# Way out of the first two FFN chunks as seven half products, placed among the way in of the next chunk

## The chip, the cores and the metric

The kernel runs on one core of one Trainium2 chip. The metric is the device time of one execution in microseconds (us); the time quoted for a kernel is the median of its timed runs. Five engines work side by side: TensorE (PE, matmuls; PEld is its loading of weights), VectorE (DVE), ScalarE (ACT), GpSimd (POOL) and SyncE (SP). DMA transfers are issued here by SP (plain loads) and by POOL (among them all that add what they bring onto what lies in SBUF). Each engine executes its own queue in order and waits on semaphores.

## The reference, cut to what matters

```python
D_MODEL, SEQ, DEPTH, D_FF = 1024, 512, 2, 2816

def swiglu(h, w_in, w_out):
    gate, up = jnp.split(h @ w_in, 2, axis=-1)
    return (jax.nn.silu(gate) * up) @ w_out

def reference(...):
    for l in range(DEPTH):
        x = x + 0.5 * swiglu(rms_norm(x, ffn1_norm[l]), ffn1_w_in[l], ffn1_w_out[l])
        h = rms_norm(x, mix_norm[l]) @ w_mix_in[l]
        ...
        x = x + y @ w_mix_out[l]
        x = x + 0.5 * swiglu(rms_norm(x, ffn2_norm[l]), ffn2_w_in[l], ffn2_w_out[l])
    return x
```

There are four FFNs in all. Everything is float32. Only the FFNs are touched by the change; the three mixers between them are not.

## The kernel before

x is held transposed in SBUF as `xT`: 8 tiles of 128 features by 512 tokens. An FFN has 2816 inner features, 22 blocks of 128, in three chunks of 8, 8 and 6 blocks (`CHUNKS`). "Way in" is the product with w_in (1024 rows; gate and up columns), "way out" the product with w_out.

**Precision.** Every float32 operand is split into a high part (an ACT cast to fp32r, line 196) and a low part (a DVE subtract, line 197), and each product is three matmuls, high by high, high by low, low by high (`mm3`, lines 208, 212, 213). `parted` splits a piece of 128x1024 weights into one of three `hl` buffers.

**Way in.** The first blocks of an FFN (`covered`: 6, in the first FFN of layer 1 4) are computed plainly in `cover`, while the normalisation is worked out. All others are done in `halved`, two blocks at a time (a *unit*), by Strassen's scheme in Winograd's form: with two columns of blocks (gate, up) by two halves of the 1024 rows by two halves of the tokens, seven half products P1 to P7 take the place of eight. Their factors are sums: of the normalised x, made once per FFN (`halves_of_x`, 14 tiles `xh*`, `xl*`), and of quarters of w_in, made per unit. A unit loads four quarters of 512 KB (line 529, SP, tiles `x0` to `x7`, two units' worth). Its sums are made by two accumulating transfers from DRAM (lines 532 and 541, POOL), one DVE add into a tile `S` (line 537), and one accumulating transfer from `S` in SBUF (line 545). A half product is 24 matmuls over 256 columns, 8 per group of three, into one PSUM bank; the weights of a half product are split two half products ahead (`LEAD`). After it comes one step of putting together on ACT or DVE (lines 597 to 619): copies out of PSUM, adds, SiLU, the products gate by up (`y`), which are split at once into `hh` and `hl`.

**Way out.** After each chunk's way in, `ffn` computes the way out of the chunk plainly: two halves of the output features, four banks each, over the chunk's inner blocks; w_out is staged by SP in pieces `st` of 512 KB (line 177), split, and multiplied in matmuls over 512 columns. After each half four DVE operations (line 370) add half of the banks to `xT`. In the last chunk the normalisation of the next stage, or the transposition of the output, hangs on this.

**Order.** The order of the instructions on each engine follows the order of the program text closely, with a scheduler's shifts at compile time. PSUM has 8 banks: `mm` 3, `sc` 2, `pt` 2, `po` 1; consecutive units and output halves take the one four and the other in turn.

Of the kernel before, what the change touches and what calls it, by code (L numbers as in the profile page):

```python
# [8 lines left out]
F32 = mybir.dt.float32  # L9
# [14 lines left out]
P = 128  # L24
T = 512
# [6 lines left out]
CHUNKS = ((0, 8), (8, 8), (16, 6))  # L32

# [11 lines left out]
class Trunk:  # L45
# [32 lines left out]
    def build_consts(self, scratch):  # L78
# [3 lines left out]
        self.ones_r = c.tile([1, P], F32, tag="ones_r", name="ones_r")  # L82
# [231 lines left out]
    def ffn(self, w_in, w_out, next_gain, covered, begin=None, out=None):  # L314

        nc = self.nc
        tc = self.tc
        with tc.tile_pool(name=self.n("ffn"), bufs=1) as fp:  # L320
            self.tt, self.tb = "g2", 2
            if begin is not None:
                x, gain, logits = begin
            for f0, nf in CHUNKS:
                self.hh = [
                    fp.tile([P, 2, T], F32R, tag=f"hh{q}", name=self.n("hh")) for q in range(nf // 2)
                ]
                self.hl = [
                    fp.tile([P, 2, T], F32R, tag=f"hl{q}", name=self.n("hl")) for q in range(nf // 2)
                ]  # L330
                halved = self.halved(fp, w_in, f0 + (covered if f0 == 0 else 0), f0 + nf, f0)
                finish = self.cover(fp, w_in, covered, begin, halved) if f0 == 0 else None
                for n, _ in enumerate(halved):

                    if f0 == 0 and n == 0:
                        finish()
                final = f0 + nf == NFF
                if final and next_gain is not None:
                    self.begin_norm(next_gain)
                last = final and out is not None  # L340
                if last:
                    xs = self.turn_x()
                for dg in range(2):
                    banks = self.next4()

                    def parts(k, kk, dg=dg):
                        r = slice((f0 + k) * P, (f0 + k + kk) * P)
                        return [w_out[r, dg * 512 : (dg + 1) * 512]]

                    spans = [slice(c, c + P) for c in (0, 128, 256, 384)]  # L350
                    self.stream(
                        [
                            (bk, slice(0, T), c) if last else (bk, c, None)
                            for bk, c in zip(banks, spans)
                        ],
                        parts, lambda k: (self.hh[k // 2][:, k % 2, :], self.hl[k // 2][:, k % 2, :]), nf,
                    )
                    if last:
                        for i in range(4):
                            o = self.xo[dg * 4 + i]  # L360
                            nc.vector.scalar_tensor_tensor(
                                out=o, in0=banks[i], scalar=0.5, in1=xs[dg * 4 + i],
                                op0=ALU.mult, op1=ALU.add,
                            )
                            nc.sync.dma_start(out[0, spans[i], dg * T : (dg + 1) * T], o)
                        continue
                    for i in range(4):
                        j = dg * 4 + i
                        xj = self.xT[:, j, :]
                        nc.vector.scalar_tensor_tensor(  # L370
                            out=xj, in0=banks[i], scalar=0.5, in1=xj,
                            op0=ALU.mult, op1=ALU.add,
                        )
                        if final and next_gain is not None:
                            self.norm_part(j, fp)

    def cover(self, fp, w_in, covered, begin, then):
# [7 lines left out]
        for f in range(0, covered, 2):  # L385
# [22 lines left out]
            if opening and begin is not None:  # L408
                nt = iter(["xh4", "xl4", "xh5", "xl5", "xh6", "xl6", "hh2", "hl2", "hh3", "hl3"])
                self.build_consts(lambda dt: fp.tile([P, T], dt, tag=next(nt), name=self.n("c")))  # L410
                self.lower_bounds(logits)
                norm()
# [16 lines left out]
    def finish(self, fp, f, i, pg, pu):  # L429
# [7 lines left out]
        nc.vector.tensor_mul(ui, gi, ui)  # L437
        hh, hl = self.hh[f // 2][:, i, :], self.hl[f // 2][:, i, :]
        nc.scalar.copy(hh, ui)
        nc.vector.tensor_sub(hl, ui, hh)  # L440

    def halves_of_x(self, fp):
# [7 lines left out]
        for q in range(4):  # L450
            xq = fp.tile([P, 2, T], F32, tag=("hh2", "hl2", "hh3", "hl3")[q], name=self.n("xn"))
# [41 lines left out]
        t1 = both(fp.tile([P, 4, H], F32, tag="S", name=self.n("T"), bufs=3))  # L493
# [9 lines left out]
    def halved(self, fp, w_in, fa, fb, f0):  # L503
# [10 lines left out]
        ORDER = ("P1", "P2", "P6", "P5", "P7", "P3", "P4")  # L514
        steps = [(f, p) for f in range(fa, fb, 2) for p in ORDER]
        raw, sums, parts = {}, {}, {}

        def quarter(f, q):
            c = (q // 2) * FF + f * P
            return w_in[(q % 2) * 512 : (q % 2) * 512 + 512, c : c + 2 * P].rearrange(  # L520
                "(k p) c -> p k c", p=P
            )

        def load(f):
            for q in (2, 3, 0, 1):
                t = self.res.tile(
                    [P, 4, 2 * P], F32, tag=f"x{4 * ((f - fa) // 2 % 2) + q}", name=self.n("w")
                )
                nc.sync.dma_start(t, quarter(f, q))
                raw[f, q] = t  # L530

            nc.gpsimd.dma_start(raw[f, 2], quarter(f, 3), accum_op=ALU.add)

        def second(f):

            t = sums[f] = fp.tile([P, 4, 2 * P], F32, tag="S", name=self.n("S"), bufs=3)
            nc.vector.tensor_add(t, raw[f, 2], raw[f, 0])

        def third(f):

            nc.gpsimd.dma_start(raw[f, 0], quarter(f, 2), accum_op=ALU.add)

        def fourth(f):

            nc.gpsimd.dma_start(raw[f, 1], sums[f], accum_op=ALU.add)

        def prepare(f, p):
            src = {
                "P1": raw[f, 0], "P2": raw[f, 1], "P6": sums.get(f), "P5": raw[f, 2],
                "P7": raw[f, 0], "P3": raw[f, 1], "P4": raw[f, 3],  # L550
            }[p]
            hi, lo = self.parted(src.rearrange("p k c -> p (k c)"), skew=SKEW_HELD)
            parts[f, p] = [a.rearrange("p (k c) -> p k c", k=4) for a in (hi, lo)]

        def product(f, p, bank, first, last, parted):
            hi, lo = parts.pop((f, p))
            xh, xl = self.xc[p]
            for i in range(2):
                acc, c = bank[:, i * H : (i + 1) * H], slice(i * P, (i + 1) * P)
                for k in range(4):  # L560
                    self.mm3(
                        acc, hi[:, k, c], lo[:, k, c], xh[:, k, :], xl[:, k, :],
                        first and i == 0 and k == 0, last and i == 1 and k == 3,
# [4 lines left out]
        LEAD = 2  # L568
        load(fa)
        for f, p in steps[:LEAD]:  # L570
            prepare(f, p)
        yield
        for n, (f, p) in enumerate(steps):
            if p == "P1" and f == fa:
                second(f)
            if p == "P1":
                third(f)
                fourth(f)
            if n + LEAD < len(steps):
                prepare(*steps[n + LEAD])  # L580
            if f + 2 < fb:
                if p == "P1":
                    load(f + 2)
                elif p == "P7":
                    second(f + 2)
            if p == "P1":
                self.ntog += 1
                a, b, c = (
                    self.bank(t) for t in (("mm", "mm", "mm"), ("sc", "sc", "pt"))[self.ntog % 2]
                )  # L590
            product(
                f, p, {"P2": c, "P5": b, "P3": b}.get(p, a), p in ("P1", "P2", "P5"),
                p in ("P2", "P3", "P4"), n == 0,
            )
            if p == "P1":
                g1 = tmp("g1")
                nc.scalar.activation(g1, a, AF.Copy, scale=-1.0)
            elif p == "P2":
                nc.vector.tensor_add(g1, g1, c)
                self.act(g1, g1, AF.Silu)  # L600
            elif p == "P6":
                g2 = tmp("g2")
                nc.scalar.activation(g2, a, AF.Copy, scale=-1.0)  # L603
            elif p == "P5":
                u2 = tmp("u2")
                nc.scalar.activation(u2, b, AF.Copy, scale=-1.0)
            elif p == "P7":
                nc.vector.tensor_add(u2, u2, a)
            elif p == "P3":
                nc.vector.tensor_add(g2, g2, b)  # L610
                self.act(g2, g2, AF.Silu)
            else:
                q = (f - f0) // 2
                pair = lambda t: t.rearrange("p (i t) -> p i t", i=2)
                y = fp.tile([P, 2, T], F32, tag="S", name=self.n("y"), bufs=3)
                nc.vector.tensor_mul(y[:, :, H:], pair(g2), pair(u2))
                nc.vector.tensor_mul(y[:, :, :H], pair(g1), pair(a))
# [725 lines left out]
```

## Time and profile before

| | us |
|---|---|
| median of 3 runs | 1919.83 (1919.29 to 1922.33) |
| the profiled execution | 1915.45 |
| its span, first to last instruction | 1913.7 |
| mean granted TensorE clock | 0.997 |

| stretch of the first FFN | us |
|---|---|
| first chunk: covered blocks and one halved unit | 0 to 108.9 |
| its way out | 108.9 to 152.3 |
| second chunk: four units of the way in | 152.3 to 228.8 |
| its way out | 228.8 to 272.3 |
| third chunk: three units | 272.3 to 329.4 |
| its way out | 329.4 to 362.1 |

The other FFNs have the same stretches (the first of layer 1 has one unit more in its first chunk). A page of the profile has the busy time of each engine, 40 slices of the span, the DMA queues, the chain of work that ended last, and the costliest groups of instructions. Durations of matmuls overlap, since matmuls are pipelined: what counts for TensorE is the distance from start to start. In the DMA figures a share of 1 means that the packets' times add up to the time of all 16 DMA engines.

### The profile page before, as it was taken

The page shows a single profiled execution, that of the slowest core. Times are in us where ns is not written, and L with a number is a line of the kernel's source. Part 1 is how long each engine was busy: PE and PEld are TensorE (multiplying, and loading weights), DVE is VectorE, ACT ScalarE, POOL GpSimd, SP SyncE. Part 2 cuts the span into 40 slices and gives each one's busy share as a digit, 9 for nine tenths or more (in the row PEclk, how much of TensorE's full clock was granted, in tenths as well). Part 3 has the DMA queues.
Part 4 walks back from the last instruction along what each step waited for, and adds up shares of the span by engine and source line. Part 5 has one row for each costly group of instructions (what it writes and reads, how often), then busy time and mean ns, then how long its engine had stood idle before and what let it go on. Part 6 is the DMA issues. An engine that isn't in the chain of part 4 may idle for free.

```text
span 1913.7 us, 30445 instructions
## 1 busy us (share of the span) xinstructions
PE 1879.9 (98%) x12240; PEld 1683.8 (88%) x12240; DVE 1280.2 (67%) x1905; ACT 928.9 (49%) x1422; POOL 142.3 (7%) x155
## 2 busy tenths in 40 slices
PE   8999999999999999999999999999999999999999
PEld 6889989899877788989989899998998787899897
DVE  7856646578787864755687466566868878656463
ACT  4434535464666542534555254355646664335252
POOL 0101100100000010201001010101000000111010
PEclk9999999999999999999999999999999999999999
DMA  5747734232323384855349376523323234858442
GB/s 143 189 142 158 193 101 99 72 94 70 78 75 93 101 229 110 195 148 111 89 146 211 105 184 170 121 72 78 89 67 84 78 101 132 207 123 202 116 100 89
DMA packets 215661, 237.56 MB, mean 124 GB/s; under 512 B 19264, under 2 KB 184128, under 8 KB 215520
## 3 DMA queue, kind: packets, MB, share of 16 engines
q1 hardware_dynamic: 175408, 183.69, 31.6%
q0 software_dynamic: 40112, 51.93, 16.9%
q8 instruction: 96, 1.57, 0.3%
q14 instruction: 45, 0.37, 0.1%
HBM read 210.87 MB, written 2.10 MB: 111 GB/s over the span
## 4 chain that ended last, share of the span: by engine, by line
PE 83%; DVE 8%; DMA 4%; ACT 3%; issue 2%; SPq 0%; POOL 0%; POOLq 0%; ACTq 0%; DVEq 0%
PE mm L208 13%; PE mm L213 13%; PE mm L212 13%; PE sc L208 8%; PE sc L212 8%; PE sc L213 8%; PE pt L208 4%; PE pt L212 4%; PE pt L213 4%; DMA w<-in_ffn_w_in_dram 3%; PE po L208 2%; PE po L213 2%; PE po L212 2%; DVE hl L197 1%; DVE xc L487 1%
## 5 line engine op out<-in xcount | busy, mean ns | idle before, releaser
L196 ACT CAST hl<-st 128x512 fp32r<-128x512 f32 (+2 forms) x268 | 222.4, 832 | 375.5 <-PE pt L213 113.0
L197 DVE TENSOR_TENSOR hl<-st,hl 128x512 fp32r<-128x512 f32 (+2 forms) x268 | 254.9, 952 | 219.0 <-ACT hl L196 217.9
L197 DVE TENSOR_TENSOR hl<-w,hl 128x1024 fp32r<-128x1024 f32 x198 | 242.6, 1226 | 228.6 <-ACT hl L196 228.4
L196 ACT CAST hl<-w 128x1024 fp32r<-128x1024 f32 x198 | 207.0, 1045 | 195.1 <-PE po L213 52.7
L208 PE MATMUL mm<-xc,hl 128*128 128x256 f32 (+1 forms) x958 | 265.3, 278 | 7.0 <-ACT g L603 7.0
L213 PE MATMUL mm<-xc,hl 128*128 128x256 f32 x952 | 265.0, 278 | 5.3 <-DVE hl L197 5.3
L212 PE MATMUL mm<-xc,hl 128*128 128x256 f32 x952 | 264.8, 278 | 0.0
L208 PE MATMUL sc<-xc,hl 128*128 128x256 f32 (+1 forms) x774 | 212.4, 276 | 0.0
L212 PE MATMUL sc<-xc,hl 128*128 128x256 f32 x768 | 212.3, 276 | 0.0
L213 PE MATMUL sc<-xc,hl 128*128 128x256 f32 x768 | 212.1, 276 | 0.0
L208 PEld LDWEIGHTS mm<-xc,hl 128*128 128x128 f32 x958 | 181.5, 189 | 8.3 <-ACT g L603 7.8
L213 PEld LDWEIGHTS mm<-xc,hl 128*128 128x128 f32 x952 | 180.3, 189 | 5.8 <-DVE hl L197 5.7
L212 PEld LDWEIGHTS mm<-xc,hl 128*128 128x128 f32 x952 | 180.2, 189 | 0.0
L208 PEld LDWEIGHTS sc<-xc,hl 128*128 128x128 f32 x774 | 145.3, 188 | 0.5
L212 PEld LDWEIGHTS sc<-xc,hl 128*128 128x128 f32 x768 | 144.2, 188 | 0.0
L213 PEld LDWEIGHTS sc<-xc,hl 128*128 128x128 f32 x768 | 144.2, 188 | 0.0
L208 PE MATMUL mm<-hl,x 128*128 128x256 f32 (+1 forms) x384 | 112.6, 293 | 0.7 <-DVE ft L298 0.4
L208 PE MATMUL mm<-x,hl 128*128 128x512 f32 x272 | 109.6, 403 | 0.0
L213 PE MATMUL mm<-hl,x 128*128 128x256 f32 (+1 forms) x384 | 107.7, 280 | 0.0
L212 PE MATMUL mm<-hl,x 128*128 128x256 f32 (+1 forms) x384 | 107.4, 280 | 0.0
L213 PE MATMUL mm<-x,hl 128*128 128x512 f32 x272 | 106.4, 391 | 0.0
L212 PE MATMUL mm<-x,hl 128*128 128x512 f32 x272 | 105.9, 389 | 0.0
(411 smaller groups left out, 4502.2 us busy)
## 6 DMA issues: line engine op xcount, KB each, us to landing
w<-in_ffn_w_in_dram SPq DMA_DIRECT2D x132, 512.0 KB, 5.1
st<-in_ffn_w_out_dram SPq DMA_DIRECT2D x88, 512.0 KB, 3.3
w<-in_ffn_w_in_dram POOLq DMA_DIRECT2D x66, 512.0 KB, 6.8
st<-in_ffn_w_in_dram SPq DMA_DIRECT2D x88, 256.0 KB, 3.1
st<-in_w_mix_in_dram SPq DMA_DIRECT2D x88, 256.0 KB, 2.7
w<-S POOLq DMA_DIRECT2D x33, 512.0 KB, 6.0
st<-in_w_mix_out_dram SPq DMA_DIRECT2D x24, 256.0 KB, 2.6
st<-in_w_mix_in_dram SPq DMA_DIRECT2D x32, 128.0 KB, 2.4
```

Of the source, the lines that this page charges most:

```text
L196: a = nc.scalar.copy(hi, src[:, c : c + w])
L197: b = nc.vector.tensor_sub(lo, src[:, c : c + w], hi)
L208: nc.tensor.matmul(acc[:, c], ah, bh[:, c], start=first and c.start == 0, stop=False, skip_group_check=True,)
L212: nc.tensor.matmul(acc, ah, bl, start=False, stop=False, skip_group_check=True)
L213: nc.tensor.matmul(acc, al, bh, start=False, stop=last, skip_group_check=True)
L487: nc.vector.tensor_sub(l, u, h)
```

## The change

The way out of chunks 0 and 1 is no longer a stage of its own. It is computed in two groups (`("O", (c, g))`, c the chunk, g the group: 256 columns of each half of w_out's 1024), each by seven half products of the same form as the way in: two halves of the chunk's 1024 inner features by two halves of the output by two halves of the tokens. `halved` now runs over the whole FFN; its list `seq` strews the 14 half products of chunk c among those of the way in of chunk c+1: 42 half products in the first mixed stretch, 35 in the second. The last chunk's way out stays as it was.

- **Inner values.** The products gate by up of chunks 0 and 1 are no longer split when made. They go into four quarters per chunk (`quarter`, 128 x 4 x 256). `moving` splits the sum that each P needs (7 per chunk, into `mh`, `ml`); the sums themselves are made by four accumulating transfers per chunk from SBUF to SBUF (`add_hidden`).
- **w_out.** Each group loads four quarters of 512 KB in turn into the tiles `x0` to `x7`, which it shares with w_in, and its sums are made by four accumulating transfers from DRAM (`add`). Its splits are those of `prepare`, seven per group.
- **xT.** After each of the 14 half products one DVE operation adds its bank to (or subtracts it from) a quarter of a group's part of `xT`. For P1, P6, P7 and P4, and for P5 and P3, the bank goes on accumulating in between.
- **Plan.** Loads and sums are issued by a table `todo`, filled ahead: at half product n the splits for n + 2, then sums on DVE, inner splits, loads, transfers that add. A load is issued 4 half products ahead of the split that needs it (`AHEAD_LOAD`), a first sum 4 ahead (`AHEAD_SUM`); later sums one half product after the split of the contents that they replace.
- **First unit of an FFN.** Its three sums that were transfers (lines 532, 541, 545) are made by DVE (`at_once`).
- `S` has two buffers and not three; `lower_bounds` works in a piece of a buffer at hand; `ones_r` is 1x1; way-in and way-out half products each take four of the PSUM banks in turn.

```diff
+ORDER_IN = ("P1", "P2", "P6", "P5", "P7", "P3", "P4")
+ORDER_OUT = ("P2", "P1", "P5", "P6", "P7", "P3", "P4")
+LEAD = 2
+AHEAD_LOAD, AHEAD_SUM = 4, 4
...
-            for f0, nf in CHUNKS:
...
-                halved = self.halved(fp, w_in, f0 + (covered if f0 == 0 else 0), f0 + nf, f0)
...
+            halved = self.halved(fp, w_in, w_out, covered)
+            finish = self.cover(fp, w_in, covered, begin, halved)
+            for n, _ in enumerate(halved):
+                if n == 0:
+                    finish()
+            f0, nf = CHUNKS[-1]
...
+        into = lambda c: [
+            ("I", f, p) for f in range(max(covered, c[0]), c[0] + c[1], 2) for p in ORDER_IN
+        ]
+        outof = lambda c: [("O", (c, g), p) for p in ORDER_OUT for g in range(2)]
+        seq = into(CHUNKS[0])
+        for c, pattern in ((0, "IIIO" + "IIO" * 12 + "IO"), (1, "IIIO" + "IOIIO" * 6 + "O")):
+            ii, oo = iter(into(CHUNKS[c + 1])), iter(outof(c))
+            seq += [next(ii if k == "I" else oo) for k in pattern]
...
+        def load(u, q, tag):
+            raw[u, q] = t = self.res.tile([P, 4, 2 * P], F32, tag=f"x{tag}", name=self.n("w"))
+            nc.sync.dma_start(t, src(u, q))
+        def add(u, q, q2):
+            nc.gpsimd.dma_start(raw[u, q], src(u, q2), accum_op=ALU.add)
+        def add_second(u):
+            nc.gpsimd.dma_start(raw[u, 1], sums[u], accum_op=ALU.add)
+        def at_once(u, name):
+            a, b, c, op = {
+                1: lambda: (raw[u, 2], raw[u, 2], raw[u, 3], ALU.add),
+                3: lambda: (raw[u, 0], sums[u], raw[u, 3], ALU.subtract),
+                4: lambda: (raw[u, 1], raw[u, 1], sums[u], ALU.add),
+            }[name]()
+            nc.vector.tensor_tensor(a, b, c, op=op)
...
+        def moving(c, p):
+            t = self.quarter(fp, c, *SUM[p])
+            hi, lo = (
+                fp.tile([P, 4, H], F32R, tag=f"m{w}", name=self.n("m"), bufs=2) for w in "hl"
+            )
+            if p in ("P1", "P7", "P4"):
+                nc.scalar.activation(hi, t, AF.Copy, scale=-1.0)
+                nc.vector.scalar_tensor_tensor(
+                    out=lo, in0=t, scalar=-1.0, in1=hi, op0=ALU.mult, op1=ALU.subtract
+                )
+            else:
+                nc.scalar.copy(hi, t)
+                nc.vector.tensor_sub(lo, t, hi)
+            mov[c, p] = hi, lo
+        def add_hidden(c, x, y):
+            x, y = (self.quarter(fp, c, *q) for q in (x, y))
+            nc.gpsimd.dma_start(x, y, accum_op=ALU.add)
...
+            split = {p: at[kind, w, p] - LEAD for p in ORDER_IN}
+            if kind == "I":
...
+                    when(m - AHEAD_SUM, 5, add, u, 2, 3)
+                    when(m, 2, second, u)
+                    when(max(m, split["P1"]), 5, add, u, 0, 2)
+                    when(max(m, split["P2"]), 6, add_second, u)
+            else:
...
+                when(split["P5"] - AHEAD_SUM, 5, add, u, 2, 3)
+                when(split["P5"] + 1, 5, add, u, 2, 0)
+                when(split["P1"] + 1, 5, add, u, 0, 2)
+                when(split["P6"] + 1, 5, add, u, 2, 1)
...
+            for p in ORDER_OUT:
+                when(n0[p] - (2 if p == "P2" else 3), 3, moving, c, p)
+            when(n0["P1"] - 2, 7, add_hidden, c, (0, 0), (0, 1))
+            when(n0["P5"] - 2, 7, add_hidden, c, (0, 0), (1, 1))
+            when(n0["P5"] - 1, 7, add_hidden, c, (0, 1), (1, 1))
+            when(n0["P6"] - 2, 7, add_hidden, c, (0, 0), (1, 0))
...
+            product(u, p, acc, p in new, p in ("P2", "P3", "P4"), n == 0)
+            if kind == "O":
+                c, g = w
+                for r, b, f in {
+                    "P2": ((0, 0, -0.5),), "P1": ((0, 0, -0.5),), "P5": ((1, 1, -0.5),),
+                    "P6": ((0, 1, -0.5),), "P7": ((1, 1, 0.5),), "P3": ((0, 1, 0.5),),
+                    "P4": ((1, 0, 0.5),),
+                }[p]:
+                    xs = self.xT[:, 4 * r + 2 * g : 4 * r + 2 * g + 2, b * H : (b + 1) * H]
+                    nc.vector.scalar_tensor_tensor(
+                        out=xs, in0=pair(acc), scalar=f, in1=xs, op0=ALU.mult, op1=ALU.add
+                    )
```

In an FFN with six covered blocks `seq` has 84 half products: 0 to 6 the unit of chunk 0, 7 to 48 the first mixed stretch, 49 to 83 the second. `split` is the position at which a half product's weights are split; m is one before that of P6; n0 is the position of group 0's half product; the second argument of `when` is the rank among what is issued at the same position.

More of the change, by code (lines that the diff above doesn't have):

```diff
@@ L377, in cover @@
+                    continue
+                for i in range(4):
+                    j = dg * 4 + i
+                    xj = self.xT[:, j, :]
+                    nc.vector.scalar_tensor_tensor(
+                        out=xj, in0=banks[i], scalar=0.5, in1=xj,
+                        op0=ALU.mult, op1=ALU.add,
+                    )
+                    if next_gain is not None:
+                        self.norm_part(j, fp)
     def cover(self, fp, w_in, covered, begin, then):
@@ L436, in finish, with quarter, hidden @@
         self.act(gi, gi, AF.Silu)
[L437 to L440, printed above, removed]
+        a, k = divmod(f + i, 4)
+        for b in range(2):
+            self.hidden(self.quarter(fp, 0, a, b)[:, k, :], *(t[:, 256 * b : 256 * b + 256] for t in (gi, ui)), a != b)
+    def quarter(self, fp, c, a, b):
+        if (c, a, b) not in self.hq:
+            self.hq[c, a, b] = fp.tile(
+                [P, 4, T // 2], F32, tag=f"r{('0123', '4512')[c][2 * a + b]}", name=self.n("hq")
+            )
+        return self.hq[c, a, b]
+    def hidden(self, out, g, u, other):
+        if other:
+            self.nc.vector.scalar_tensor_tensor(
+                out=out, in0=g, scalar=-1.0, in1=u, op0=ALU.mult, op1=ALU.mult
+            )
+        else:
+            self.nc.vector.tensor_mul(out, g, u)
     def halves_of_x(self, fp):
@@ L501, in halves_of_x, with halved @@
         yield part("P4", minus(b21, b21, t2))
-    def halved(self, fp, w_in, fa, fb, f0):
+    def halved(self, fp, w_in, w_out, covered):
         nc = self.nc
         H = T // 2
[L514 to L521, printed above, removed]
-            )
[L524 to L527, printed above, removed]
-                )
[L529 to L557, printed above, removed]
@@ new lines, in halved, with when, src @@
+        at = {s: n for n, s in enumerate(seq)}
+        raw, sums, parts, mov = {}, {}, {}, {}
+        first = covered
+        todo = {}
+        def when(n, rank, fn, *args):
+            todo.setdefault(max(n, -1), []).append((rank, fn, args))
+        def src(u, q):
+            kind, w = u
+            if kind == "I":
+                r, c, v = (q % 2) * 512, (q // 2) * FF + w * P, w_in
+            else:
+                r, c, v = (CHUNKS[w[0]][0] + 4 * (q % 2)) * P, (q // 2) * 512 + w[1] * 256, w_out
+            return v[r : r + 512, c : c + 2 * P].rearrange("(k p) c -> p k c", p=P)
@@ L558, in product @@
+        def product(u, p, bank, start, stop, parted):
+            hi, lo = parts.pop((u, p))
+            xh, xl = self.xc[p] if u[0] == "I" else mov[u[1][0], p]
             for i in range(2):
@@ L562, in product @@
                         acc, hi[:, k, c], lo[:, k, c], xh[:, k, :], xl[:, k, :],
-                        first and i == 0 and k == 0, last and i == 1 and k == 3,
+                        start and i == 0 and k == 0, stop and i == 1 and k == 3,
                         parted and i == 0 and k == 0,
@@ L567, in halved @@
         tmp = lambda tag: fp.tile([P, T], F32, tag=tag, name=self.n(tag), bufs=2)
[L568 to L571, printed above, removed]
-        yield
[L573 to L597, printed above, removed]
+        pair = lambda t: t.rearrange("p (i t) -> p i t", i=2)
@@ new lines, in lower_bounds, with take @@
+        used = 0
+        def take(*shape):
+            nonlocal used
+            n = shape[0] * (shape[1] if len(shape) > 1 else 1)
+            t = scratch[:, used : used + n]
+            used += n
+            return t.rearrange("p (l r) -> p l r", r=2) if len(shape) > 1 else t
+        lg = take(DEPTH, 2)
+        nc.sync.dma_start(lg, logits.rearrange("l (r p) -> p l r", p=P))
+        m = take(2)
+        nc.vector.tensor_copy(m, lg[:, 0, :])
+        for l in range(1, DEPTH):
+            nc.vector.tensor_max(m, m, lg[:, l, :])
@@ new lines, in lower_bounds @@
+        e = take(DEPTH, 2)
+        for l in range(DEPTH):
+            nc.vector.tensor_sub(e[:, l, :], lg[:, l, :], m)
+        self.act(e, e, AF.Exp)
+        s = take(2)
+        nc.vector.tensor_copy(s, e[:, 0, :])
+        for l in range(1, DEPTH):
+            nc.vector.tensor_add(s, s, e[:, l, :])
+        nc.vector.reciprocal(s, s)
+        for l in range(DEPTH):
+            nc.vector.tensor_mul(e[:, l, :], e[:, l, :], s)
+        self.lb = self.const.tile([P, DEPTH, 2], F32, tag="lb", name="lb")
@@ L662, in lower_bounds @@
+        self.lb1 = self.const.tile([P, DEPTH, 2], F32, tag="lb1", name="lb1")
+        cum = take(2)
+        nc.vector.tensor_copy(cum, e[:, 0, :])
+        for l in range(DEPTH):
+            if l:
+                nc.vector.tensor_add(cum, cum, e[:, l, :])
+            d = take(2)
+            nc.vector.tensor_sub(d, cum, e[:, 0, :])
             nc.vector.tensor_scalar(
-                one, self.lb1, scalar1=0.0, scalar2=-1e30, op0=ALU.is_equal, op1=ALU.mult
+                self.lb[:, l, :], d, scalar1=0.0, scalar2=1.0, op0=ALU.max, op1=ALU.min
```

251 lines of the change are left out of this document (151 added, 100 removed).

## The prediction

> **What bounds the kernel now.** I read the page's busy shares first, then busy time by stretch for one way out and one way in, then TensorE's timeline, and last stretches of two or three microseconds for the DMA engines.
>
> ```profile
> PE 1879.9 (98%) x12240; PEld 1683.8 (88%) x12240; DVE 1280.2 (67%) x1905; ACT 928.9 (49%) x1422; POOL 142.3 (7%) x155
> ...
> q1 hardware_dynamic: 175408, 183.69, 31.6%
> q0 software_dynamic: 40112, 51.93, 16.9%
> ```
>
> TensorE is busy 98% of the span; nothing that leaves its instruction count alone can gain much. q1 holds plain loads, q0 POOL's transfers, nearly all of them accumulating.
>
> ```profile
> 108.90:152.30 43.40, 43.40 (x193) 35.92 (x192) 18.54 (x20) 9.37 (x9) 2.17 (x2) 1.00 0.38 105
> 152.30:228.80 76.50, 76.50 (x675) 76.48 (x674) 52.30 (x53) 42.33 (x51) 11.70 (x10) 1.00 0.82 189
> ```
>
> Columns: length; busy time and count of PE, PEld, DVE, ACT, POOL; granted clock; DMA share; GB/s. The first line is the way out of one chunk of eight, the second the way in of the next. TensorE never pauses in either. But the DMA share is 0.38 in one and 0.82 in the other: the way in already asks much of the DMA engines, and the way out is where they rest.
>
> ```profile
> 150.05 0.39 PE L213 MATMUL mm<-hh,hl 128*128 128x512 f32 x1
> 150.28 0.39 PE L208 MATMUL mm<-hh,hl 128*128 128x512 f32 x1
> ...
> 153.92 0.28 PE L212 MATMUL sc<-xc,hl 128*128 128x256 f32 x1
> 154.04 0.28 PE L213 MATMUL sc<-xc,hl 128*128 128x256 f32 x1
> ```
>
> Durations overlap; starts count. A product over 512 columns starts every 0.227 us (43.4/192 is 0.226), one over 256 every 0.1133 us (76.5/675). Half products are no dearer per column.
>
> **TensorE's term.** One chunk's way out goes from 192 products of 512 columns, 43.5 us, to 14 half products of 24 matmuls of 256: 336 x 0.1133 = 38.1 us. That is 5.4 us per chunk, two chunks in each of four FFNs: 8 x 5.4 = **-43.5 us**. A half product lasts 24 x 0.1133 = 2.72 us; I call that a step, and number steps from the first way-in half product of an FFN with six covered blocks.
>
> **VectorE and ScalarE.** Per chunk the change drops 8 splits of staged w_out, 4 splits of inner values and 8 updates of xT, and adds 14 splits of w_out sums, 7 of inner sums and 14 updates. A split is 1.05 us on ACT and 1.22 on DVE (a following row starts after 1.13), an update 0.69: DVE +9 x 1.22 + 6 x 0.69 = +15 us, ACT +9.5 us. Cover: DVE spends 52.3 of 76.5 us in the way in, 13 us per unit of seven steps. With four units less their inner splits (47.5), 21 splits (23.7) and 14 updates at 0.6 (8.4), the first mixed stretch of 42 steps has 80 of 114 us; the second, of 35 steps, about 71 of 95. The densest steps (58 to 60) ask 8.6 us in 8.2, and weights are split two steps ahead. I take 0; without that lead it would be 0.4 us eight times, 3 us. The rearranged constants (lower_bounds, ones_r) do the same work under the opening's matmuls: 0.
>
> **Opening of each FFN.** The first unit now sums on DVE instead of by transfer.
>
> ```profile
> 99.00 0.58 PE L208 MATMUL mm<-xc,hl 128*128 128x256 f32 x1 [6.06 <-ACT g L603]
> ...
> 1028.00 0.41 PE L208 MATMUL mm<-xc,hl 128*128 128x256 f32 x1
> 1028.21 0.41 PE L212 MATMUL mm<-xc,hl 128*128 128x256 f32 x1
> ```
>
> Idle times before first units come to 6.06 + 1.84 + 0.31 + 0.26 + 3.43 + 0.38 = 12.3 us. After the 6.06 and 3.43 us ones matmuls start every 0.213 us for some fifteen of them: 1.5 us more each. All gone would be -15 us. Against it, three sums of 1.22 us come onto DVE in the first three steps, beside the delayed finish of the covered blocks, 8 operations near 0.6: some 14 us where 8 pass. Unhidden they cost 3.6 x 4 = +15 us. Neither is nearer; I take **0**, ends -15 and +15.
>
> **The transfers.** All sums of w_out and of inner values go through POOL's queue. Per way out: 8 loads as before, plus 8 adds from DRAM (two groups of four) and 4 adds of inner quarters from SBUF. Each way-in unit keeps 4 loads, 2 DRAM adds, 1 SBUF add. What one costs with the engines full:
>
> ```profile
> 168.00:170.00 2.00, 2.00 (x20) 2.00 (x19) 1.24 (x2) 1.03 (x2) 1.15 (x1) 1.00 1.09 377
> 172.00:174.00 2.00, 2.00 (x20) 2.00 (x20) 2.00 (x3) 1.15 (x2) 0.46 (x1) 1.00 1.26 200
> 174.50:176.00 1.50, 1.50 (x15) 1.50 (x15) 1.47 (x2) 1.50 (x3) 0.00 (x0) 1.00 1.05 210
> 92.00:95.00 3.00, 0.94 (x9) 0.74 (x7) 0.00 (x0) 0.00 (x0) 0.00 (x0) 1.00 1.17 233
> ```
>
> By the issues around them these are loads alone, DRAM adds alone (L541, 194 GB/s over three such stretches), the SBUF add alone (L545), and both kinds at once. So 524 KB cost 1.4 us as a load, 2.7 us as a DRAM add, 2.5 us as an SBUF add. First mixed stretch: 24 x 1.4 + 16 x 2.7 + 8 x 2.5 = 97 of 114 us; second: 20 x 1.4 + 14 x 2.7 + 7 x 2.5 = 83 of 95. The mean fits; what decides is where the adds bunch, because a sum has only about four steps (10.9 us) until its split.
>
> An add that waits for nothing lands 6.0 us after issue (L541's median), so 3.3 us beside its 2.7. Cast and subtract before a product take 2.3 us.
>
> Second stretch, POOL's issues by step: 55 one SBUF; 56 three DRAM; 58 two; 60 one DRAM, two SBUF; 61 one and one; 63 one; 65 one SBUF; 66 one; 68 two. The tenth of these, group 0's second sum into its third tile (issued at step 61 before the inner one), is wanted for step 67. From step 55: 7 x 2.7 + 3 x 2.5 = 26.4, four loads 5.6, fixed 3.3, split 2.3: 37.6 us, while step 67 is due at 12 x 2.72 = 32.6. Late by 5.0. Group 1's (step 63) follows 5.2 later, plus two loads 2.8: 45.6 against step 69's 38.1: late by 7.5. The next unit's sum (68), 10.6 + 1.4 later and with 1.2 us for DVE's sum, is 4.4 late, within what was lost.
>
> First stretch, from step 13: twelve adds to step 23 (8 DRAM, 4 SBUF) 31.6, seven loads 9.8, 3.3, a sum 1.2, a split 2.3: 48.2 against step 30's 46.2, late 2.0. The add of step 27 for step 33: 10.6 more and no sum: 57.6 against 54.4, late **3.2**.
>
> Loads and adds at once run worse than their prices added. In 92 to 95 us, if the packets alternate, 233 GB/s is about 114 each, and 114/194 + 114/377 = 0.89. Over some 14 us of mixing that is about 1.5 us more in each stretch. So 4.7 + 9.0 = 13.7 us per FFN, and one stall over 3.4 us, 1.5 more: **15.2 us**, four times +61 us.
>
> Who waits: ACT's cast waits for the add, and behind it in ACT's queue stand later casts and copies of finished products out of PSUM; a late way-in sum holds DVE, and with it the xT updates and the silu chain.
>
> Bounds. If loads cost adds nothing, every step above is in time (step 67: 32.0 against 32.6): 0. The page's share puts an add at 0.169 x 1914 / 99 = 3.27 us: 15 + 13 us late, two surcharges, 31 us per FFN. I take 15.2, nearest the rows of the same kinds of transfer.
>
> In sentences of its own: the Trainium skill (DMA: Bandwidth & Descriptors, Anatomy of one DMA) gives about 2.0 us plus bytes/436 GB/s, an estimated 1.2 us of moving for 524 KB; 48 transfers would be 58 of 114 us and nothing would be late. The trace disagrees for accumulating ones, 2.7 us. The same page (Issuing engines are not separate DMA queues) says that transfers from all issuing engines share the 16 DMA engines, and the mixed row agrees.
>
> **Sum.** The profiled execution took 1915.5 us (span 1913.7). -43.5 + 0 + 0 + 61 = +17, so 1933. The runs' median is 1919.8, 4.4 above; the same difference on it gives **1936 us**.
>
> **Rivals.**
> 1. *The transfers keep up.* For it: mean demand is under 90%, TensorE never waits now at 0.82 share, and shares above 1 show packets overlapping. Against: the bunches above. Nothing late gives 1919.8 - 43.5 = **1876 us**. A page's rule leads here too: the estimate of 1.2 us above. It decides as long as lateness with surcharge stays under 9.9 us per FFN, where the gain falls to 3.8 us. 0.32.
> 2. *Break-even*, 9.9 to 11.8 us late: about 1920. 0.06.
> 3. *Each add costs the page's share*, 3.27 us: (31 - 10.9) x 4 = +80, **2000 us**. For it: three adds and little else filled 86 to 96 us. 0.05.
> 4. *DVE becomes the bound*, the transfers keeping up: its bunches of 0.4 us and the opening's +15 give 1876 + 3 + 15 = **1894 us**. Against: 75% load. 0.05.
> 5. *That the halves are not cheaper*: excluded by 675 rows of the same form at 0.1133 us.
>
> **Chances.** Forecast 0.52, rivals 0.32, 0.06, 0.05, 0.05. A measurement can tell some 0.2% (3.8 us) from no change. Faster 0.32 + 0.05 = 0.37, same 0.06, slower 0.57. Lateness from 12 to 25 us per FFN puts the forecast's own case at 1924 to 1977; the whole range needs both signs, 1882 to 1988, and leaves out the end of rival 1 where under 1.5 us per FFN is late (some 0.12) and rival 3 (0.05).
>
> **What would show it.** TensorE instructions up by 8 x 144 = 1152. Right: idle TensorE in stretches of 1 to 5 us in the last third of each mixed stretch, ended by the split (L197's successor), with ACT waiting for DMA and POOL adds landing 15 us or more after issue; DMA share near 1 there. Wrong: adds landing within some 10 us throughout, or the mixed stretches lasting 114 and 95 us: then 1876. Idle time ended by DVE while no DMA is late would speak for rival 4.

## The result and the profile after

The changed kernel takes **1953.69 us** (median of 4 runs, 1952.10 to 1955.14) against 1920.73 before (4 runs): ratio 1.0171, interval 1.0154 to 1.0189. It is slower by 33 us, where the forecast had 16. The profiled execution took 1955.04 us, its span is 1953.3.

The page of the changed kernel: busy time of the engines, the two DMA queues, the group of DVE's sum `S` (`second`, line 579), and the transfers that POOL issues (last column: median us from issue to landing).

```profile
PE 1875.0 (96%) x13384; PEld 1735.3 (89%) x13384; DVE 1404.8 (72%) x2048; ACT 1000.8 (51%) x1483; POOL 239.8 (12%) x239
...
q1 hardware_dynamic: 191792, 183.69, 31.5%
q0 software_dynamic: 73712, 95.97, 30.0%
...
L579 DVE TENSOR_TENSOR S<-w,w 128x1024 f32<-128x1024 f32 x33 | 40.4, 1223 | 105.6 <-DMA w<-in_ffn_w_in_dram 105.4
...
w<-in_ffn_w_out_dram POOLq DMA_DIRECT2D x64, 512.0 KB, 8.9
w<-in_ffn_w_in_dram POOLq DMA_DIRECT2D x58, 512.0 KB, 7.8
...
hq<-hq POOLq DMA_DIRECT2D x32, 512.0 KB, 9.4
w<-S POOLq DMA_DIRECT2D x29, 512.0 KB, 9.2
```

TensorE has 1144 instructions more, as announced (1152), and less busy time. But it is busy 96% of a longer span, no longer 98%. By the medians no kind of POOL's transfers takes 15 us to land, and no single one of them does (the longest takes 14.2). The line that stands out is DVE's sum: it takes 40.4 us in all, and DVE stood still for 105.6 us in front of it (32.5 in the kernel before), waiting for transfers of w_in.

The timeline of the changed kernel at one such place, first DVE, then POOL, then TensorE (start, duration, instruction; in brackets the idle time before it and what ended that):

```profile
186.99 1.22 DVE L618 TENSOR_TENSOR m<-hq,m 128x1024 fp32r<-128x1024 f32 x1
195.20 1.22 DVE L579 TENSOR_TENSOR S<-w,w 128x1024 f32<-128x1024 f32 x1 [6.99 <-DMA w<-in_ffn_w_in_dram]
196.34 1.22 DVE L203 TENSOR_TENSOR hl<-w,hl 128x1024 fp32r<-128x1024 f32 x1
```

```profile
187.13 1.29 POOL L572 DMA_DIRECT2D w<-in_ffn_w_in_dram  x1 [6.45 <-DVE hl L203]
```

```profile
192.67 0.28 PE L214 MATMUL po<-xc,hl 128*128 128x256 f32 x1
192.78 0.28 PE L218 MATMUL po<-xc,hl 128*128 128x256 f32 x1
197.61 0.58 PE L219 MATMUL po<-xc,hl 128*128 128x256 f32 x1 [4.55 <-DVE hl L203]
197.99 0.41 PE L214 MATMUL po<-xc,hl 128*128 128x256 f32 x1
198.20 0.41 PE L218 MATMUL po<-xc,hl 128*128 128x256 f32 x1
198.42 0.41 PE L219 MATMUL po<-xc,hl 128*128 128x256 f32 x1
```

The sum's transfer is issued at 187.13 and lands 8 us later, which is ordinary. What is not ordinary is that DVE already stands at the sum. Behind it in DVE's queue is the low part of a weight split (196.34) that TensorE needs first; TensorE waits 4.55 us for it and then starts matmuls every 0.21 us, not every 0.1133, for a while.

**The time by FFN.** For each FFN I take the distance from the start of its first half-product matmul to the start of its last. The work in it is known: after the change 84 half products of 2.72 us, 228.5 us (third FFN 91, 247.5); before it 56 and two ways out of 43.4, 239.1 us (third 63, 258.2). What is over is lateness, idle time and time at half rate together:

| lateness, us | FFN 1 | 2 | 3 | 4 | sum |
|---|---|---|---|---|---|
| before | 8.4 | 3.7 | 6.5 | 1.7 | 20.3 |
| after | 27.0 | 27.2 | 21.9 | 25.9 | 102.0 |

The work shrinks by 10.6 us in three FFNs and 10.7 in the third, 42.5 us. With the profiled execution of before: 1915.5 - 42.5 - 20.3 + 102.0 = 1954.7, against 1955.0. The question is where the 102 us come from.

The order of DVE's instructions around another such sum of the first FFN, from the built program (position, line, instruction):

```
after   176 L203 hl_1091 <- w_779      (a split)
after   177 L579 S_1352  <- w_1127, w_1158
after   178 L203 hl_1122 <- w_841      (the next split)
...     seven further splits
after   194 L203 hl_1383 <- S_1352     (the split that needs S)
```

In the program text the sum stands right ahead of its own split. The compile-time scheduler has put it eight splits, so eight half products, earlier in DVE's queue.

### The profile page after: what moved, and what is told of

It is laid out like the page before. It is cut to its first block, busy times and chain, and to the rows that moved or that the text cites. A ratio compares the mean times of both kernels' runs of the same rounds, so it can differ in the third digit from the quotient of the medians.

```text
span 1953.3 us, 33198 instructions
## 1 busy us (share of the span) xinstructions
PE 1875.0 (96%) x13384; PEld 1735.3 (89%) x13384; DVE 1404.8 (72%) x2048; ACT 1000.8 (51%) x1483; POOL 239.8 (12%) x239
## 3 DMA queue, kind: packets, MB, share of 16 engines
q1 hardware_dynamic: 191792, 183.69, 31.5%
## 4 chain that ended last, share of the span: by engine, by line
PE 67%; DVE 13%; DMA 11%; issue 5%; ACT 4%; POOL 0%; SPq 0%; DVEq 0%; ACTq 0%; POOLq 0%
PE mm L214 10%; PE mm L219 10%; PE mm L218 10%; DMA w<-in_ffn_w_in_dram 7%; DVE hl L203 4%; PE sc L219 4%; PE sc L214 4%; PE sc L218 4%; PE pt L219 4%; PE pt L214 4%; PE pt L218 4%; DMA hq<-hq 3%; PE po L219 3%; PE po L214 2%; PE po L218 2%
## 5 line engine op out<-in xcount | busy, mean ns | idle before, releaser
L202 ACT CAST hl<-w 128x1024 fp32r<-128x1024 f32 x310 | 324.1, 1047 | 345.1 <-PE pt L219 80.9
L203 DVE TENSOR_TENSOR hl<-w,hl 128x1024 fp32r<-128x1024 f32 x310 | 378.4, 1222 | 135.8 <-ACT hl L202 135.7
L219 PE MATMUL mm<-xc,hl 128*128 128x256 f32 x1008 | 281.3, 279 | 1.5 <-DVE hl L203 1.4
L218 PE MATMUL mm<-xc,hl 128*128 128x256 f32 x1008 | 281.2, 279 | 0.0
L203 DVE TENSOR_TENSOR hl<-st,hl 128x512 fp32r<-128x512 f32 (+2 forms) x204 | 176.2, 865 | 114.6 <-ACT hl L202 113.5
L202 ACT CAST hl<-st 128x512 fp32r<-128x512 f32 (+2 forms) x204 | 155.0, 762 | 186.8 <-PE mm L219 64.5
L572 POOL DMA_DIRECT2D w<-in_ffn_w_in_dram x58 | 76.6, 1340 | 802.5 <-DVE hl L203 350.0
L219 PE MATMUL po<-xc,hl 128*128 128x256 f32 x336 | 98.6, 293 | 23.3 <-DVE hl L203 23.3
L579 DVE TENSOR_TENSOR S<-w,w 128x1024 f32<-128x1024 f32 x33 | 40.4, 1223 | 105.6 <-DMA w<-in_ffn_w_in_dram 105.4
L219 PE MATMUL sc<-m,hl 128*128 128x256 f32 x336 | 98.2, 292 | 18.7 <-DVE hl L203 18.7
L572 POOL DMA_DIRECT2D w<-in_ffn_w_out_dram x64 | 86.7, 1397 | 196.5 <-DVE hl L203 138.9
L218 PE MATMUL po<-xc,hl 128*128 128x256 f32 x336 | 97.4, 290 | 0.0
```

What stands on the lines that cost most here:

```text
L202: a = nc.scalar.copy(hi, src[:, c : c + w])
L203: b = nc.vector.tensor_sub(lo, src[:, c : c + w], hi)
L218: nc.tensor.matmul(acc, ah, bl, start=False, stop=False, skip_group_check=True)
L219: nc.tensor.matmul(acc, al, bh, start=False, stop=last, skip_group_check=True)
L572: nc.gpsimd.dma_start(raw[u, q], src(u, q2), accum_op=ALU.add)
L579: nc.vector.tensor_add(t, raw[u, 2], raw[u, 0])
```

## The experiments

**Sums at their planned place, and thin transfers.** Theory A: DVE's early sums cost the time. Theory B: the transfers' load does, as the forecast had it. The first kernel holds each `S` behind the split of its own half product, by an order that costs no semaphore:

```diff
 def parted(...):      # after tensor_sub
+    self.split = b.ins.name
 def second(u):
-    nc.vector.tensor_add(t, raw[u, 2], raw[u, 0])
+    i = nc.vector.tensor_add(t, raw[u, 2], raw[u, 0])
+    if u != ("I", first):
+        self.tc.add_manual_dep(i.ins, self.split, NOSYNC, reason="sum after the split")
```

> The changed kernel with one thing undone: each unit's sum S on DVE stands right behind the split of its own step, no longer some four steps ahead of it in DVE's queue. Theory A (DVE stands in its queue at an early sum until the transfer lands: 13 stops, 53 us of TensorE idle and some 20 us of half clock after them): nearly all of this goes, 1953.7 - 65 = about 1888 us, surely under 1905. Theory B (the transfers' queue is late whatever the order, 13.7 us and a surcharge per FFN, as forecast): the wait only moves from the sum to the splits, 1936 us, not under 1925.

1887.19 us (1882.12 to 1889.54), ratio to before 0.9825, interval 0.9806 to 0.9844: theory A. An order on one instruction per unit makes the change a gain: 66.5 us less than the changed kernel. In its trace DVE waits 0.1 us in all ahead of `S`. With this order the scheduler also exchanges some neighbours in POOL's queue; what that is worth alone was not run.

The second has the same order and brings only 32 of 256 columns in every accumulating transfer; the third has the thin transfers in the changed kernel's order.

```diff
-            nc.gpsimd.dma_start(raw[u, q], src(u, q2), accum_op=ALU.add)
+            nc.gpsimd.dma_start(raw[u, q][:, :, :32], src(u, q2)[:, :, :32], accum_op=ALU.add)
```

> The same order as the run before it, but every accumulating transfer of the FFNs brings 32 of its 256 columns (the other columns of the sums are left out); the instructions of the engines are the same. It measures what the transfers' load still costs once the order is mended. Theory A: little, within 5 us of the run before it. Theory B: the lateness goes, 1936 - 61 = 1875 us, some 60 us below the run before it.

1852.49 us (1851.74 to 1853.24). Both theories missed: 34.7 us below the pinned kernel, neither under 5 nor 60. The transfers' load costs something here, a little over half of the forecast's 61.

> The changed kernel with the early sums in its order, and every accumulating transfer of the FFNs cut to 32 of 256 columns (the other columns of the sums are left out). Theory A: an early sum still waits, but only for the fixed part of a transfer, some 3 to 4 us in place of 7 to 8, less than the two steps by which splits are ahead: most stops fall under 1 us, 1885 to 1905 us. Theory B: nothing is late, 1875 us, the same as the run with the order mended and thin transfers.

1866.35 us (1857.92 to 1872.22), lower than either theory said. The early place costs 13.9 us with thin transfers. A w_out transfer then lands 3.3 us after issue and not 8.9, and DVE waits 31.5 us ahead of `S` and not 105.6.

**The opening alone.** The kernel before, in which only the first unit of each FFN makes its three sums on DVE (`at_once`):

```diff
-            nc.gpsimd.dma_start(raw[f, 2], quarter(f, 3), accum_op=ALU.add)
+            if not (f == fa and f0 == 0):
+                nc.gpsimd.dma_start(raw[f, 2], quarter(f, 3), accum_op=ALU.add)
...
+            opening = f == fa and f0 == 0
...
+                if opening:
+                    nc.vector.tensor_add(raw[f, 2], raw[f, 2], raw[f, 3])
...
-            if p == "P1":
+            if p == "P1" and not opening:
                 third(f)
                 fourth(f)
...
+            if opening and p == "P2":
+                nc.vector.tensor_sub(raw[f, 0], sums[f], raw[f, 3])
+            if opening and p == "P6":
+                nc.vector.tensor_add(raw[f, 1], raw[f, 1], sums[f])
```

> The kernel before with only the opening's part of the change: the first halved unit of each FFN makes its three sums on DVE in place of accumulating transfers. My forecast took 0 for this part (ends -15 and +15). The trace after has 4 us of idle TensorE there where before had 12.3 and two half-clock stretches of 1.3 and 1.6 us: theory A' says 1920.7 - 10 = 1911 us. Rival: the gain in that trace came from other loads and the unit alone gains nothing, 1919 to 1922 us.

1904.95 us (1903.33 to 1906.17), ratio 0.992, interval 0.9907 to 0.9933: 16 us gained, more than the 10 that theory A' had. The lateness of its FFNs is 4.7, 0.6, 2.6 and 0.6 us, 8.5 in place of 20.3.

**Which transfers cost the 34.7 us.** What waits in the pinned kernel, by its list of waits (total us, times, longest):

```profile
POOL hq L626 <- DMA hq<-hq: 66.6, 8, 10.6
...
ACT hl L202 <- DMA w<-in_ffn_w_in_dram: 40.1, 16, 5.9
...
ACT m L620 <- DMA hq<-hq: 25.1, 7, 5.7
...
ACT hl L202 <- DMA w<-in_ffn_w_out_dram: 16.1, 5, 4.2
```

ACT's casts wait for late tiles of every kind (the rows of `w` hold plain loads too). Four kernels, all with the pinned order, lighten the queue: the inner sums made by DVE; those and the sum from `S` made by DVE; thin transfers for w_out's sums only; thin ones for w_in's sums from DRAM only.

```diff
 def add_hidden(c, x, y):
-    nc.gpsimd.dma_start(x, y, accum_op=ALU.add)
+    nc.vector.tensor_add(x, x, y)
 def add_second(u):                                   # the second kernel only
-    nc.gpsimd.dma_start(raw[u, 1], sums[u], accum_op=ALU.add)
+    nc.vector.tensor_add(raw[u, 1], raw[u, 1], sums[u])
```

> The kernel with the pinned sums, and the four sums of inner values per chunk made by DVE (32 x 1.22 = 39 us more of DVE work) and not by transfers (8 x 2.5 = 20 us of DMA time less per FFN, a sixth of the accumulating transfers' time). 34.7 us hang on the load of the transfers there. Theory A, a common backlog: the transfers are late because they queue behind each other, so less of any kind helps all: 1865 to 1872 us. Theory B, each kind is late by its own short notice, whatever the others do: only the stops at inner sums go (three of 4.7 to 5.7 us on ACT, with little on TensorE): 1880 to 1885. Theory C, DVE's slack is not where the sums fall: 1887 or more, with idle time of TensorE ended by DVE.

**1853.11 us** (1851.92 to 1853.49), ratio 0.9653, interval 0.9639 to 0.9667. This is the fastest kernel that computes everything: 3.5% below before, and lower than any theory said.

> As before, and DVE makes the way-in units' second sum from S too (29 x 1.22 = 35 us more of DVE work, in all 75 on 1405, some 78% of the span), so that only accumulating transfers from DRAM are left. Theory A (common backlog): a third of the accumulating transfers' time is gone, 1855 to 1862 us. Theory B (each by its own notice): 1878 to 1884. Theory C (DVE full at the dense steps): 1887 or more.

1869.92 us (1853.36 to 1870.79), in the range of no theory. The profiled execution is the fastest of the five, with lateness in one FFN only (0.8 us). What the other runs lost is in no profile and stays open.

> The kernel with the pinned sums, where the 64 accumulating transfers of w_out bring 32 of 256 columns (the sums of w_out are left out in the rest). Theory A (common backlog): some 43 of 120 us per FFN of accumulating time fall away, and with them nearly all lateness: 1852 to 1860 us. Theory B (each by its own notice): only the stops at w_out's sums go, and what this and the thinned w_in save adds up to no more than the 34.7 us that all thinned saved: 1870 to 1880.

1852.54 us (1852.28 to 1854.08). In this kernel and the next the transfers named bring 32 of 256 columns, by the edit of the thin transfers above.

> The kernel with the pinned sums, where the 58 accumulating transfers of w_in from DRAM bring 32 of 256 columns (the sums of w_in are left out in the rest). Theory A (common backlog): some 39 of 120 us per FFN fall away: 1853 to 1862 us, so that this and the thinned w_out together save more than the 34.7 us that all thinned saved. Theory B (each by its own notice): the stops at w_in's first sums go, the largest ones on TensorE: 1866 to 1874, and the savings of both add up to no more than 34.7 us.

1853.41 us (1852.64 to 1857.29). Each of three kinds, moved to DVE or thinned alone, gives back all of the 34 to 35 us: 34.1 (inner sums), 34.7 (w_out) and 33.8 (w_in). That is theory A, a common backlog. The first FFN's half products of the kernel with inner sums on DVE, by stretch (length; busy time and count of PE, PEld, DVE, ACT, POOL; clock; DMA share; GB/s), and after it the same part of the changed kernel:

```profile
81.30:309.80 228.50, 228.50 (x2018) 228.50 (x2017) 186.99 (x195) 128.81 (x144) 43.95 (x36) 1.00 0.84 184
```

```profile
82.40:337.90 255.50, 238.35 (x2017) 237.14 (x2017) 177.80 (x187) 127.01 (x144) 50.87 (x44) 0.96 0.84 181
```

TensorE is busy without a pause in the first, with DVE at 187 of 228.5 us. The DMA share is 0.84 in both, the kernel without lateness and the one that is 27 us late here; in the pinned kernel, 12.3 us late here, it is 0.89. The mean doesn't tell which kernel is late.

**How the backlog comes about.** The next kernel leaves the load as it is and gives more notice:

```diff
-AHEAD_LOAD, AHEAD_SUM = 4, 4
+AHEAD_LOAD, AHEAD_SUM = 4, 6
```

> The pinned kernel with all transfers, where first sums are issued six and not four half products ahead of their split (their loads two earlier too); the load of the queue is the same. If the 34.7 us are lateness of bunched transfers against short notice, 5.4 us more notice takes most of it: 1853 to 1866 us. If the engines are full over whole stretches, notice changes little: 1880 us or more.

1917.29 us (1913.74 to 1922.52): 30 us *slower* than the pinned kernel, against both expectations. TensorE's longest stop is at the same half product in every FFN, number 23 (30 in the third, which has one unit more ahead of it): 7.00, 6.79, 6.29 and 6.84 us, where the pinned kernel has 3.83, 0.32, 3.02 and 0.92. In the first FFN, the pinned kernel first:

```profile
148.40 0.39 PE L215 MATMUL mm<-xc,hl 128*128 128x256 f32 x1 [3.83 <-ACT hl L202]
```

```profile
152.01 0.58 PE L215 MATMUL mm<-xc,hl 128*128 128x256 f32 x1 [7.00 <-ACT hl L202]
```

The cast that it waits for needs the later sum of a way-in unit (`add(u, 0, 2)`). POOL's timeline shows that transfer as the line ahead of `w<-S`. In the pinned kernel:

```profile
118.29 0.86 POOL L626 DMA_DIRECT2D hq<-hq  x1 [10.63 <-DMA hq<-hq]
122.46 1.30 POOL L573 DMA_DIRECT2D w<-in_ffn_w_out_dram  x1 [3.31 <-DVE hl L203]
127.78 2.60 POOL L573 DMA_DIRECT2D w<-in_ffn_w_out_dram  x2 [4.02 <-DMA w<-in_ffn_w_out_dram]
129.29 2.01 POOL L626 DMA_DIRECT2D hq<-hq  x1
130.93 1.69 POOL L573 DMA_DIRECT2D w<-in_ffn_w_out_dram  x1
132.30 1.63 POOL L573 DMA_DIRECT2D w<-in_ffn_w_in_dram  x1
133.05 1.80 POOL L576 DMA_DIRECT2D w<-S  x1
```

With more notice:

```profile
116.29 1.30 POOL L573 DMA_DIRECT2D w<-in_ffn_w_out_dram  x1 [0.56 <-issue]
128.64 2.60 POOL L573 DMA_DIRECT2D w<-in_ffn_w_out_dram  x2 [11.04 <-DVE hl L203]
130.14 2.01 POOL L626 DMA_DIRECT2D hq<-hq  x1
130.69 2.79 POOL L573 DMA_DIRECT2D w<-in_ffn_w_in_dram  x1
131.44 3.35 POOL L573 DMA_DIRECT2D w<-in_ffn_w_out_dram  x1
132.51 3.59 POOL L573 DMA_DIRECT2D w<-in_ffn_w_in_dram  x1
133.26 3.76 POOL L576 DMA_DIRECT2D w<-S  x1
```

POOL issues in order too. A transfer whose buffer or operand isn't free holds all behind it, and they leave together: six within 5.3 us in the pinned kernel, seven within 4.6 us here (a line with x2 is two). In both the first of the bunch is a first sum of w_out, and it goes when the load of its own tile has landed (here at 128.05 us, 0.6 us earlier), so not earlier for the notice. The DMA engines' busy tenths from 125 to 150 us in the kernel with more notice, and what its issues there took to land:

```profile
DMA  9999310009899999999999899999999999999999
...
w<-in_ffn_w_in_dram POOLq DMA_DIRECT2D x2, 512.0 KB, 15.8
w<-S POOLq DMA_DIRECT2D x1, 512.0 KB, 20.1
```

The DMA engines rest for some 2.5 us at the head of the bunch and then are full for the rest of the stretch. The bunch lands in the order of its issue, a transfer every 2.5 to 4.2 us, so its last ones are the latest. The sum that TensorE stops for is issued at 132.30 us in the pinned kernel and at 132.51 here, but lands 14.9 us later there and 18.3 here (7.4 with the inner sums on DVE, where TensorE doesn't stop). What is new ahead of it is the line at 130.69, the first sum of the next way-in unit, which takes 3.4 us of the landings: about what TensorE's stop grows by (7.00 for 3.83). By the plan this sum belongs to step 21 and the two issues behind it to steps 18 and 17; in the built program the scheduler has put it ahead of them. So more notice let a sum that is wanted later go ahead of one that is wanted at once. All four FFNs have this transfer in this place with more notice, and none in the pinned kernel; in the second and fourth the bunch also leaves over 2 us later than there. No run moves this one transfer alone, so this is read from the traces and not shown by an experiment.

**Early sums without a backlog.** The changed kernel's order, the inner sums on DVE:

> The changed kernel, sums not pinned, with only the four sums of inner values per chunk moved from transfers to DVE. Theory A: what DVE loses at a sum placed early is the lateness of that sum's transfer, and this is mostly the common backlog, so the early place costs little once the backlog is gone, as with all transfers thin (13.9 us above the pinned one): 1862 to 1872 us. Theory B: the early place costs by itself what it cost in the changed kernel (66.5 us): 1853 + 66, some 1920 us, with stops of DVE of 6 us or more at L579 as before.

1917.49 us (1909.55 to 1931.14), ratio to before 0.9994 (0.9973 to 1.0015). Theory B: the early place costs 64.4 us here (1917.5 - 1853.1), as it cost 66.5 with the full queue. (The profiled execution is the fastest of 11; by lateness it is 57.5 us here and 69.5 there.) DVE's wait ahead of `S` is 66.5 us here and was 31.5 with thin transfers: those landed sooner, and an emptier queue alone doesn't bring as much.

## Why the prediction was wrong, point by point

The lateness of each kernel, as in the table above, adds up with the same base (1915.5 - 42.5 - 20.3 = 1852.7):

| kernel | lateness, us | 1852.7 + lateness | profiled execution |
|---|---|---|---|
| after | 102.0 | 1954.7 | 1955.0 |
| pinned | 32.5 | 1885.2 | 1885.4 |
| pinned, inner sums on DVE | 0.0 | 1852.7 | 1853.5 |
| after's order, inner sums on DVE | 57.5 | 1910.2 | 1909.6 |
| pinned, more notice | 69.5 | 1922.2 | 1922.3 |

- **TensorE, -43.5: right.** 42.5 us by the lengths above; the matmuls of half products start every 0.1133 us beside all the rest (228.5 us for 84).
- **VectorE and ScalarE, 0: right as a matter of work.** With 39 us more of DVE work TensorE still never waits in the half products. Rival 4 falls, though its sign came: in the changed kernel TensorE's idle time is ended by DVE (L203). But there DVE stood, for 105.6 us ahead of `S`, and was not full.
- **Opening, 0 with ends of -15 and +15: mis-sized.** It is worth -16 us alone. Sums that hang on no transfer end the idle time ahead of first units, and what they add to DVE is hidden. Of before's 20.3 us of lateness 8.5 are left with this part alone, and none in the pinned kernel with the inner sums on DVE.
- **The transfers, +61: the failed step, in two halves that err in opposite directions.** The backlog, in which ACT's casts wait for late sums, is real, but costs 32.5 us in the profile (34.7 by medians). It doesn't come in the last third of the mixed stretches by the prices of 2.7 and 2.5 us; in the first FFN the largest stop is at step 23 ((144.29 - 81.7)/2.72), behind the bunch that POOL let go after it had stood at a dependent inner sum (10.63 us) and at w_out's. The working counted issues by the plan and never asked what each waits for at the head of POOL's queue. Nor is the built queue the plan: that inner sum belongs to step 21, and the scheduler has put it ahead of four sums of w_out from steps 15 to 19.
- **What is missing there:** "a sum has only about four steps (10.9 us) until its split". For the way-in units this took the plan's step for the place in DVE's queue. In the built program DVE comes to `S` up to eight half products ahead, as at 187 us right after its transfer has left, so that a transfer which lands in time for its split can still stop DVE for most of its 8 us. The "who waits" of the prediction named the victim ("a late way-in sum holds DVE") but needed lateness for it; none is needed. It costs 69.5 us (102.0 - 32.5).
- **The sum.** Forecast 1933 for the profiled execution, measured 1955.0: +1.0 (TensorE), -20.3 (before's idle time), -28.5 (backlog 32.5 for 61), +69.5 (early sums) make +21.7 of the 22.1. The direction was right by luck: errors of opposite sign, -48.8 and +69.5, partly cancel.
- **Rival 1**, transfers that keep up, is what the kernel with the inner sums on DVE became: 1853 and not 1876, most of it by the 20.3 us of idle time that went as well.

## What to carry to other kernels

An engine's queue has no plan, only an order: where an instruction waits for a transfer, look up its place in the built order before pricing the transfer, and pin it behind the work that must not wait (here 66 us for an order without a semaphore). A queue of transfers has the same rule: count what each issue waits for, and what stands in front of the one that is wanted next, since a held head makes bunches out of a mean load that fits, and issuing earlier can make them worse (30 us here). Near the edge a small part of the load can be worth everything: moving a sixth of it to DVE bought back all 34 us here, and so did thinning either of two other kinds.

## What the runs showed of the hardware

- **The clock.** In the changed kernel TensorE stopped 13 times for 2.5 us or more in the FFNs; after 12 of them matmuls of 256 columns started every 0.213 us, 14 to 26 of them, which cost 22 us in all. Its granted clock is 0.985, against 1.0 in every kernel without such stretches. The shortest stop with it was 2.51 us, and one of 3.33 had none. In the pinned kernel some 18 such matmuls follow two stops of 1.36 and 0.92 us, one right after the other. The Trainium skill (TensorE: Matmul & The Clock Gate, Part 1: The HAM clock gate) gives half rate after at least one idle window of about 3.4 us; the traces have it below that too, so the length of a stop alone doesn't decide.
- **Where a transfer waits.** The Trainium skill (DMA: Bandwidth & Descriptors, Anatomy of one DMA) says that a semaphore is waited for by the issuing sequencer, ahead of dispatch. The trace with more notice agrees: POOL stood 11.04 us ahead of one transfer, the DMA engines came to rest at about 128 us while seven were still held, and all seven left from 128.64 us on.
- **Size and landing.** An accumulating transfer of 64 KB of w_out landed 3.3 us after issue, one of 512 KB 8.9. A wait that comes too early is paid by landing time: DVE stood 105.6 us ahead of `S` with the large ones and 31.5 with the small.
